# Early gathers behind splits, spread rows, first gates in two parts, and single-head routing in a transformer block with an expert layer

## The chip, the cores and the metric

The kernel runs on one core of one Trainium2 chip. The metric is the device time of one execution in microseconds; a kernel's time is the median of several. The engines are named as in the profile: PE is TensorE (matmul), DVE is VectorE, ACT is ScalarE, POOL is GpSimd, SP is SyncE, which here only issues DMAs.

## The reference

One residual block on x of 512 tokens by 1024 columns, all in float32. The first half (a gated MLP on token blocks and a banded attention, added to x through `w_out`) isn't touched by the change. The second half is a layer of small experts:

```
q = (xb @ w_query).reshape(128, 8, 2, 128)            # 8 heads, two halves
sc = einsum('thpd,hpkd->thpk', q, sub_keys)           # 128 keys in each half
s_top, i_top = top_k(sc, 16)
cand = s_top[0][:, None] + s_top[1][None, :]          # 256 pairs, index i0 * 128 + i1
best, pos = top_k(cand, 16);  eidx = cand_idx[pos];  g = softmax(best)
u = expert_u[eidx];  h = gelu(einsum('thkd,td->thk', u, xb))
out = einsum('thk,thkd->td', g * h, expert_v[eidx])
```

There are 128 x 128 = 16384 experts; each token takes 16 in each of 8 heads, 128 rows of `expert_u` and 128 of `expert_v`.

## The kernel before

**Two ways to the same sum.** For the first tile of 128 tokens (the gathered tile) the chosen rows are fetched with indirect DMAs, 128 gathers of u rows (L876) and 128 of v rows (L887); DVE multiplies (L878) and accumulates (L889). For the other 384 tokens (the dense tiles) all experts are computed: first products `u . x` for 128 chunks of 128 experts, gelu (`act`, L547), times a gate that is zero for experts not chosen, then second products with `expert_v`. The last 64 of the dense tokens have no first products: their 128 u rows per token are gathered early (64 gathers of 128 rows, `rowe`, L480), DVE dots them (L489), and the result goes into their gates. So first products have 320 columns and second products 384.

**Splits.** Each weight tile of 512 KB comes by a DMA on SP into `raw` (three buffers); ACT makes `hi` (L124), and DVE or POOL `lo` = raw - hi (L125). A product is three matmuls, hi by hi, hi by lo and lo by hi (L140 to L142). A k-step is the three matmuls of one of the 8 slices of 128 rows; a first product of one chunk of 128 experts takes 8 k-steps, and the kernel takes the chunks in pairs (64 pairs, numbered c; "chunk" below means a pair, and `AHEAD` = 23 and `LAST` count pairs).

**Stages.** Up to some 225 us in the profile the first half of the block. To 460 us *routing* of the dense tiles, head by head: `candidates(h)` makes q and scores on PE with weight splits on POOL, two or three first products as filling, and the top 16 keys on DVE; `pairs` and `choose` of head h-1 find the best 16 pairs (L593, L600 to L619). POOL issues the early gathers here: `indices_early` brings a head's indices into place with a DMA and a cast (`eui`, L495, L496), then `gather_early` issues up to six at a time into `rowe` buffers.

From 460 to 620 us the *gate stage*, written out by hand for PE, DVE, ACT and POOL: 48 steps of 8 tokens. In each, DVE compares an iota with the second index (`bm`, L747), POOL multiplies by the gate (L749), DVE and ACT compare with the first index (`am`, L757, L761, L763), and two steps later PE multiplies the two (L770, 16 matmuls in the profile, shown as x8 in the order): the result is the gate of all 16384 experts for these tokens. ACT copies it into `gst` (L773), and after every second step a store of 1 MB goes from ACT's queue to DRAM (`gd<-gst`, L776, 24 in all). Until step 32 each step also issues one early gather on POOL and dots one row on DVE as long as there are any; in the profile these are 22. Between the products PE works at k-steps of first products, as many as are left up to chunk `AHEAD - LAST`, spread evenly over the steps that are left, rounded up; their tiles are split as they are used.

Then the *passage*: the remaining first products up to chunk 23, and for the first chunk of second products the gates' load from DRAM (`gc<-gd`, L910, 1536 KB for 8 chunks of 128 experts, issued by POOL; later ones by SP), `act` times gate on DVE (L923, in place), `wh` and `wl` (L924, L925; L934 and L935 for the 64 columns that come straight from the gates) and the matmuls L945, L946 and L949.

To the end the *second product*: 64 chunks, PE's order by hand, with the first products of chunk c+23 behind chunk c. At every sixth chunk `route_gathered` selects for two heads of the gathered tile (`PARTS` = 4; scores `s0d` by a DMA into `sc0`, top 16 on DVE, the tree copied by POOL at L600), and the gathers and their DVE work are spread over the chunks, with four buffers `row`, of which each selection takes one as well.

**Order.** Outside the parts by hand a scheduler sets each engine's order from the order of the program, priorities and buffers; `tc.issue_after(x)` keeps what is inside behind instruction x. An engine takes its instructions strictly in order, and so does each queue of DMAs.

Of the kernel before, what the change touches and what calls it, by code (L numbers as in the profile page):

```python
# [8 lines left out]
F32 = mybir.dt.float32  # L9
# [5 lines left out]
ALU = mybir.AluOpType  # L15
# [4 lines left out]
P = 128  # L20
D = 1024
# [5 lines left out]
NH = 8  # L27
TOPK = 16
# [27 lines left out]
RAW = 3  # L56
HI = 5
LO = 5
ROW = 4
ROWA = 6  # L60
ROWE = 4
LAGE = 3
BRIDGE = 8
EARLY = 6
LEAD = 2
ON_ACT = 2
AHEAD = 23
LAST = 3
HELD = 2
SOME = 15  # L70
FILL = (2, 2, 2, 2, 3, 3, 3, 3)
DELAY = 6
SLACK = 4
PRIO = 400
PARTS = 4
ROUTE = 6
GB = 8
TC = 8
TG = 16
NG = NDT // TG  # L80


def bcast_rows(ap, n):
# [4 lines left out]
def hybrid_block(tc, x, ln1, w_in, gng, wsT, bsb, qkg, bias, w_out, ln2, wq, skT, uT, ud, vd, out):  # L88
    nc = tc.nc
    ctx = ExitStack()  # L90
    with ctx:
# [19 lines left out]
        nc.gpsimd.iota(iota_k, pattern=[[1, P]], base=0, channel_multiplier=0,  # L111
                       allow_small_or_imprecise_dtypes=True)

        loads = []

        def load_split(src, eng=nc.vector, **dims):

            raw = big("raw", F32, RAW)
            hi = big("hi", F32R, HI)
            lo = big("lo", F32R, LO)  # L120
            fold = (lambda v: v.rearrange("p (a b) -> p a b", **dims)) if dims else (lambda v: v)
            load = nc.sync.dma_start(fold(raw), src)
            loads[:] = [getattr(load, "ins", load)]
            nc.scalar.activation(hi, raw, AF.Copy)  # L124
            eng.tensor_tensor(lo, raw, hi.bitcast(F32), op=ALU.subtract)  # L125
            return fold(hi), fold(lo)

        def chunk_of(w, c, ch=CH, eng=nc.vector):
# [337 lines left out]
        row = rq.tile([P, D], F32, name="rowe", tag="rowe", bufs=ROWA)  # L466
# [9 lines left out]
        def gather_early(n, rows_of, n_rows):  # L476

            for j in early[:n]:
                row = rows_of.tile([P, D], F32, name="rowe", tag="rowe", bufs=n_rows)
                nc.gpsimd.indirect_dma_start(out=row, out_offset=None, in_=ud,  # L480
                                             in_offset=bass.IndirectOffsetOnAxis(ap=eui[:, j:j + 1], axis=0))
                issued.append((j, row))
            del early[:n]
# [14 lines left out]
        def ready_early(h):  # L498
            early.extend(range(h * HK, (h + 1) * HK))
# [42 lines left out]
        def multiply_tile(whole=False):  # L542
            multiply_some(KT, whole)
# [122 lines left out]
        def indices_of(t):  # L666

            ei = gat.tile([P, NH * TOPK], I32, name="ei", tag="ei", bufs=1)
            ii = gat.tile([P, 2, NH * TOPK], I32, name="ii", tag="ii", bufs=1)
            ff = gat.tile([P, 2, NH * TOPK], F32, name="ff", tag="ff", bufs=2)  # L670
# [8 lines left out]
            pass  # L679
        cands = []  # L680
        for h in range(NH + 1):
            if h > 1:
                ready_early(h - 2)
            dots_early(0)
            gather_early(EARLY, rq, ROWA)
            if h < NH:
                cands.append(candidates(h))
            else:
                for i, _ in enumerate(first_products(sum(FILL) + BC, BRIDGE, nc.gpsimd, True)):
                    behind.append(done[0])  # L690
            if h > 0:
                hs = slice((h - 1) * TOPK, h * TOPK)
                ps = pa()
                mask = ps[:, 0:6 * ND * TOPK].bitcast(U32)
                tree = rq.tile([P, ND, TOPK, 32], F32, name="tree", tag="tree", bufs=1)
                with tc.issue_after(behind[BRIDGE // 2 - 1]) if behind else ExitStack():
                    cand = pairs(rq, *cands.pop(0), ND, ps[:, 6 * ND * TOPK:8 * ND * TOPK])
                choose(rq, cand, ND, gate[:, GT:, hs], eidx[:, GT:, hs], mask, tree, nc.scalar.copy)
                indices_early(h - 1)
            if h == 4:  # L700

                nc.gpsimd.tensor_copy(xch, xbh[:, :, T0:T0 + NDU])
                nc.gpsimd.tensor_copy(xcl, xbl[:, :, T0:T0 + NDU])
# [10 lines left out]
            split_next()  # L714
        with tc.issue_after(behind[-3]):
            softmax(rq, gate[:, GT:, :].rearrange("p t (h k) -> p (t h) k", k=TOPK), ND * NH)
        ready_early(NH - 1)
        dots_early(0)
        routing.close()
        xn_ctx.close()  # L720


        gd = dram.tile([NB // GB, P, NG, GB * TG], F32, name="gd")
        more.append(ctx.enter_context(tc.tile_pool(name="more", bufs=1)))
        gp_ctx = ExitStack()
        gp = gp_ctx.enter_context(tc.tile_pool(name="gp", bufs=1))
# [46 lines left out]
                nc.scalar.copy(st[:, :, t0:t0 + 4], ps.rearrange("p (t b) -> p b t", b=NB))  # L773

        def store(n, st):
            nc.scalar.dma_start(gd[:, :, n, :].rearrange("q p f -> p q f"),  # L776
                                st.rearrange("p (q b) t -> p q (b t)", b=GB))

        def rows_of_v(c):

# [7 lines left out]
        engines = {getattr(mybir.EngineType, e) for e in ("PE", "DVE", "Activation", "Pool")}  # L788
        own = steps - UX // TC
        with tc.manual_schedule(engines=engines):  # L790
            multiply_tile()
            gs[0] = gates_of(GT, ff.pop(0))
            split_next()
            multiply_tile()
            for n in range(steps + LEAD):
                t, c = divmod(n, per)
                if n < steps:
                    bms[n] = second_one_hot(gs[t], c)
                if n >= LEAD:
                    m = n - LEAD  # L800
                    if m * TC % TG == 0:
                        st = gp.tile([P, NB, TG], F32, name="gst", tag="gst", bufs=2)
                    products(ams.pop(m), bms.pop(m), m % per, st)
                    if (m + 1) * TC % TG == 0:
                        store(m * TC // TG, st)
                while begun:
                    activate_tile()
                if n < steps:
                    ams[n] = first_one_hot(gs[t], c)
                if n < own - 7:  # L810
                    gather_early(1, gp, ROWE)
# [12 lines left out]
                if n == own - 3:  # L824

                    late = gates_of(GT + t, ff.pop(t))
                if n == own - 1:
                    gs[t] = late

                made = len(ready) * KT + (KT - open_tile[4] if open_tile else 0)  # L830
                left = (AHEAD - LAST) * BC * KT - split * KT + made
                some = -(-left // (steps + LEAD - n))
                multiply_some(some)
                while split < (AHEAD - LAST) * BC + HELD and len(ready) < HELD:
                    split_next(nc.vector if split % 2 else nc.gpsimd)
# [10 lines left out]
        gat_ctx.close()  # L846


        ep = ctx.enter_context(tc.tile_pool(name="ep", bufs=1))

        xb0 = ep.tile([P, D], F32, name="xb0")
        nc.gpsimd.dma_start(xb0, xbd[0])
        acc0 = ep.tile([P, D], F32, name="acc0")
# [2 lines left out]
        def route_gathered(b):  # L856
# [5 lines left out]
            for h in range(n):  # L862
                for p2 in range(2):
# [3 lines left out]
            mask = ep.tile([P, 6 * n * TOPK], U32, name="mask", tag="mask", bufs=1)  # L867
            tree = ep.tile([P, D], F32, name="tree", tag="row", bufs=ROW)
            choose(ep, pairs(ep, top, pos, n), n, best, to, mask,
                   tree.rearrange("p (h k m) -> p h k m", h=n, k=TOPK))  # L870
            softmax(ep, best, n)
            nc.vector.tensor_copy(eint[:, hs], eidx[:, 0, hs])

# [29 lines left out]

        acx = px()
        accs = [[acx[:, 0:512], acx[:, 512:]]] + [[pa() for _ in range(2)] for _ in range(ND - 1)]
        gcs = {}

        def load_gates(q, eng):
            gcs[q] = ep.tile([P, NG, GB, TG], F32, name="gc", tag="gc", bufs=2)
            eng.dma_start(gcs[q].rearrange("p n b t -> p (n b t)"), gd[q].rearrange("p n f -> p (n f)"))  # L910

        def second_product(c):
            w = weights.pop(c) if c in weights else rows_of_v(c)
            if c == 0:
                load_gates(0, nc.gpsimd)
# [105 lines left out]
```

## Time and profile before

| | |
|---|---|
| median of 3 runs | 1485.53 us (1485.14 to 1485.57) |
| the profiled execution | 1489.41 us |
| its span, first to last instruction | 1487.5 us |
| mean granted PE clock | 0.983 |
| busy PE, DVE, POOL, ACT | 1410.3, 1143.3, 682.8, 651.7 us |
| DMA moved | 396.77 MB |

The profile is one execution on the chip. A busy time counts each engine's own instructions; idle time is put down to the instruction or DMA that ended it. Names are those of the program's buffers: `lo<-raw,hi` is an instruction that writes `lo` and reads `raw` and `hi`. The prediction shows the lines that it uses. PE matmuls overlap, so that the time from one start to the next tells what one costs, not its length.

### The profile page before, as it was taken

The numbers are of one execution on the slowest core, as the hardware profiler recorded it, in microseconds if no ns is written. First come the engines' busy times: TensorE is split into PE (matmuls) and PEld (weight loads), VectorE is DVE, ScalarE is ACT, GpSimd is POOL, SyncE is SP. The second block draws the span as 40 slices with busy tenths as digits, with TensorE's granted clock in tenths as the row PEclk, the third lists the DMA queues.
The fourth block names the chain that finished last, engine by engine and source line by source line (L and its number), as shares of the span: only waits on it lengthen the run. The fifth ranks groups of instructions, "written<-read, shape, count | busy, mean of one in ns | idle before, by whom it ended". The sixth has DMA issues, their size and how long they took to land.

```text
span 1487.5 us, 21777 instructions
## 1 busy us (share of the span) xinstructions
PE 1410.3 (95%) x7804; PEld 1238.6 (83%) x7804; DVE 1143.3 (77%) x2397; ACT 651.7 (44%) x1124; POOL 682.8 (46%) x464
## 2 busy tenths in 40 slices
PE   7999999999889878889989999999999999999998
PEld 6886688998788778888978888888989999888877
DVE  4437543698987979588989879898898888788783
ACT  5447534443345667643434334343343333433331
POOL 0000007577776877404435455465465544444430
PEclk9999999999989999999999999999999999999999
DMA  5352136387765986868879899999999999889892
GB/s 184 114 184 71 61 111 201 131 285 259 260 211 163 333 283 199 244 224 326 302 280 338 300 357 341 337 355 344 379 349 358 359 332 372 333 287 325 319 365 94
DMA packets 161419, 396.77 MB, mean 267 GB/s; under 512 B 12304, under 2 KB 74528, under 8 KB 159264
## 3 DMA queue, kind: packets, MB, share of 16 engines
q1 hardware_dynamic: 62992, 197.42, 37.4%
q0 software_dynamic: 47488, 171.50, 31.3%
q10 hardware_dynamic: 50832, 26.48, 6.2%
q8 instruction: 61, 1.00, 0.3%
q14 instruction: 46, 0.38, 0.1%
HBM read 363.86 MB, written 31.46 MB: 266 GB/s over the span
## 4 chain that ended last, share of the span: by engine, by line
PE 48%; DMA 17%; DVE 11%; issue 10%; POOL 8%; ACT 4%; ACTq 0%; SPq 0%; DVEq 0%; POOLq 0%
PE pu L140 7%; PE pu L142 7%; PE pu L141 7%; DMA row<-in_vd,eint 4%; PE pa L945 4%; PE pa L946 4%; PE pa L949 4%; DMA row<-in_ud,eint 3%; DMA raw<-in_uT 3%; DVE lo L125 3%; POOL lo L125 3%; DMA gc<-gd 3%; PE pa L140 2%; PE pa L142 2%; PE pa L141 2%
## 5 line engine op out<-in xcount | busy, mean ns | idle before, releaser
L124 ACT ACTIVATE hi<-raw 128x1024 fp32r<-128x1024 f32 x300 | 316.9, 1059 | 551.1 <-DMA raw<-in_vd 239.2
L125 DVE TENSOR_TENSOR lo<-raw,hi 128x1024 fp32r<-128x1024 f32 x249 | 305.0, 1226 | 107.9 <-ACT hi L124 106.8
L887 POOL DMA_INDIRECT row<-in_vd,eint x128 | 197.4, 1542 | 184.3 <-DVE acc L889 158.8
L876 POOL DMA_INDIRECT row<-in_ud,eint x128 | 185.9, 1452 | 202.8 <-DVE row L878 146.5
L140 PE MATMUL pu<-xch,hi 128*128 128x320 f32 x784 | 248.2, 317 | 2.4 <-ACT act L547 2.3
L142 PE MATMUL pu<-xch,lo 128*128 128x320 f32 x784 | 242.8, 310 | 0.8 <-DVE lo L125 0.6
L141 PE MATMUL pu<-xcl,hi 128*128 128x320 f32 x784 | 242.9, 310 | 0.0
L945 PE MATMUL pa<-hi,wh 128*128 128x512 f32 x512 | 200.6, 392 | 0.0
L946 PE MATMUL pa<-lo,wh 128*128 128x512 f32 x512 | 200.0, 391 | 0.0
L889 DVE SCALAR_TENSOR_TENSOR acc<-row,hw,acc 128x1024 f32<-128x1024 f32 x128 | 164.9, 1288 | 43.2 <-DMA row<-in_vd,eint 42.9
L878 DVE SCALAR_TENSOR_TENSOR row<-row,xb 128x1024 f32<-128x1024 f32 x128 | 155.7, 1218 | 31.3 <-DMA row<-in_ud,eint 31.2
L125 POOL TENSOR_TENSOR lo<-raw,hi 128x1024 fp32r<-128x1024 f32 x51 | 123.5, 2435 | 81.5 <-ACT hi L124 76.8
L949 PE MATMUL pa<-hi,wl 128*128 128x512 f32 x512 | 157.7, 389 | 0.0
L140 PEld LDWEIGHTS pu<-xch,hi 128*128 128x128 f32 x784 | 148.8, 190 | 5.9 <-ACT act L547 4.4
L142 PEld LDWEIGHTS pu<-xch,lo 128*128 128x128 f32 x784 | 148.5, 189 | 1.9 <-DVE lo L125 1.3
L141 PEld LDWEIGHTS pu<-xcl,hi 128*128 128x128 f32 x784 | 148.8, 190 | 1.4
L770 PE MATMUL pa<-bm,am 128*128 128x128 f32 x768 | 105.1, 291 | 27.3 <-POOL bm L749 12.7
L770 PEld LDWEIGHTS pa<-bm,am 128*128 128x128 f32 x768 | 97.6, 203 | 34.7 <-POOL bm L749 26.0
L945 PEld LDWEIGHTS pa<-hi,wh 128*128 128x128 f32 x512 | 96.7, 189 | 20.6
L946 PEld LDWEIGHTS pa<-lo,wh 128*128 128x128 f32 x512 | 96.6, 189 | 20.4
L949 PEld LDWEIGHTS pa<-hi,wl 128*128 128x128 f32 x512 | 96.3, 188 | 20.5
L946 PE MATMUL px<-lo,wh 128*128 128x512 f32 x256 | 101.6, 397 | 7.9 <-DVE lo L125 7.9
(218 smaller groups left out, 2664.1 us busy)
## 6 DMA issues: line engine op xcount, KB each, us to landing
raw<-in_uT SPq DMA_DIRECT2D x128, 512.0 KB, 5.8
raw<-in_vd SPq DMA_DIRECT2D x128, 512.0 KB, 5.6
gd<-gst ACTq DMA_DIRECT2D x24, 1024.0 KB, 6.6
gc<-gd SPq DMA_DIRECT2D x15, 1536.0 KB, 10.7
raw<-in_w_in SPq DMA_DIRECT2D x20, 512.0 KB, 4.5
raw<-in_wq SPq DMA_DIRECT2D x16, 512.0 KB, 3.7
raw<-in_w_out SPq DMA_DIRECT2D x8, 512.0 KB, 4.2
bt<-in_bias SPq DMA_DIRECT2D x8, 256.0 KB, 7.3
```

What stands on the lines that cost most here:

```text
L124: nc.scalar.activation(hi, raw, AF.Copy)
L125: eng.tensor_tensor(lo, raw, hi.bitcast(F32), op=ALU.subtract)
L140: nc.tensor.matmul(ps, lh[0], rh[0], start=first, stop=False)
L141: nc.tensor.matmul(ps, lh[0], rh[1], start=False, stop=False)
L142: nc.tensor.matmul(ps, lh[1], rh[0], start=False, stop=last)
L770: nc.tensor.matmul(ps[:, i * P:(i + 1) * P], am[:, 4 * q + i, :], bm[:, 4 * q + i, :], start=True, stop=True)
L876: nc.gpsimd.indirect_dma_start(out=row, out_offset=None, in_=ud, in_offset=bass.IndirectOffsetOnAxis(ap=eint[:, j:j + 1], axis=0))
L887: nc.gpsimd.indirect_dma_start(out=row, out_offset=None, in_=vd, in_offset=bass.IndirectOffsetOnAxis(ap=eint[:, j:j + 1], axis=0))
L889: nc.vector.scalar_tensor_tensor(acc0, row, hw[:, j:j + 1], acc0, op0=ALU.mult, op1=ALU.add)
L945: nc.tensor.matmul(accs[t][half], wh[:, b, tok], w[b][0][:, ds_], start=first, stop=False)
L946: nc.tensor.matmul(accs[t][half], wh[:, b, tok], w[b][1][:, ds_], start=False, stop=False)
L949: nc.tensor.matmul(accs[t][half], wl[:, b, tok], w[b][0][:, ds_], start=False, stop=last)
```

## The change

It has five parts.

1. *Gathers behind splits.* In the routing loop the index DMA and cast and the early gathers of head h-2 are placed behind the first POOL split of head h (`splits`), where before the gathers stood ahead of it in the program and the indices at the end of the turn before. All `rowe` buffers now come from one pool with six buffers; before the gate stage had four of its own. One gather is issued ahead of the gate stage. `pairs` and `choose` of the last head wait for different first products.
2. *Gate-stage rows spread.* A gather is issued in two of three steps up to step 32, not in every one until none is left.
3. *`LAST` 3 to 2.* One chunk more, two tiles of 8 k-steps, gets its first products within the gate stage, and the passage has as many fewer.
4. *First gates.* The stored gates are two DRAM tensors, groups 0 to 19 (the 320 columns) and 20 to 23. The first block's large part (1280 KB) is loaded from POOL at step 46 into memory that comes free at step 39; the small part (256 KB) after the last stores. All later blocks are two loads on SP as well. The two buffers `gc` are in two pools.
5. *Single heads and five buffers.* `PARTS` 8 and `ROUTE` 3: one head at every third chunk. `ROW` 5.

```diff
-ROW = 4
+ROW = 5
-LAST = 3
+LAST = 2
-PARTS = 4
-ROUTE = 6
+PARTS = 8
+ROUTE = 3
+GROUPS = ((0, NDU // TG), (NDU // TG, NG))
...
-            if h > 1:
-                ready_early(h - 2)
             dots_early(0)
-            gather_early(EARLY, rq, ROWA)
             if h < NH:
                 cands.append(candidates(h))
...
+            if h > 1:
+                with tc.issue_after(splits[0]):
+                    indices_early(h - 2)
+                    ready_early(h - 2)
+                    gather_early(EARLY, gat, ROWA)
...
-                indices_early(h - 1)
...
+        def load_gates(q, eng, parts=range(len(GROUPS))):
+            if q not in gcs:
+                gcs[q] = gcp[q % 2].tile([P, NG, GB, TG], F32, name="gc", tag="gc", bufs=1)
+            for i in parts:
+                n0, n1 = GROUPS[i]
+                eng.dma_start(gcs[q][:, n0:n1].rearrange("p n b t -> p (n b t)"),
+                              gds[i][q].rearrange("p n f -> p (n f)"))
...
-                if n < own - 7:
-                    gather_early(1, gp, ROWE)
+                if n < own - 7 and n % 3 < 2:
+                    gather_early(1, gat, ROWA)
...
                 if n == own - 1:
                     gs[t] = late
+
+                    gat_ctx.close()
+                    gcp = [ctx.enter_context(tc.tile_pool(name="gcp", bufs=1, side="right"))]
+                if n == steps - 2:
+                    load_gates(0, nc.gpsimd, range(1))
...
+        gcp.append(ep)
+
+        load_gates(0, nc.gpsimd, range(1, len(GROUPS)))
```

Line numbers of the changed kernel are a few higher: L480 is L482 there, L495 is L497, L770 is L775, L910 is L792, L923 is L938, L924 is L939.

**POOL in routing, fourth to sixth block of early gathers.** Before, from the fourth index DMA on (`lo` is a split, `rowe` a gather):

```order
L495 DMA eui<-eidx 64x8
L496 CAST eui<-eidx 64x8
L480 DMA rowe<-in_ud,eui 128x1024 x6
L125 TENSOR_TENSOR lo<-raw,hi 128x1024
L480 DMA rowe<-in_ud,eui 128x1024 x2
L125 TENSOR_TENSOR lo<-raw,hi 128x1024 x3
L495 DMA eui<-eidx 64x8
L496 CAST eui<-eidx 64x8
L125 TENSOR_TENSOR lo<-raw,hi 128x1024
L480 DMA rowe<-in_ud,eui 128x1024 x4
```

Now, from the same index DMA on:

```order
L497 DMA eui<-eidx 64x8
L498 CAST eui<-eidx 64x8
L125 TENSOR_TENSOR lo<-raw,hi 128x1024
L482 DMA rowe<-in_ud,eui 128x1024 x6
L125 TENSOR_TENSOR lo<-raw,hi 128x1024 x3
L497 DMA eui<-eidx 64x8
L498 CAST eui<-eidx 64x8
L125 TENSOR_TENSOR lo<-raw,hi 128x1024 x2
L482 DMA rowe<-in_ud,eui 128x1024 x6
L125 TENSOR_TENSOR lo<-raw,hi 128x1024 x3
```

The first three blocks (6 and 2, 8, and 8 gathers, each behind one split) stand the same in both; in the fourth the six gathers went from ahead of a split to behind it, in the fifth behind two. In all, 43 gathers now stand ahead of the gate stage's steps, 42 before.

**PE in the gate stage, at the thirteenth to fifteenth step's products.** Before, one k-step between the products of two steps (`pa` is a gate product, `pu` a first product):

```order
L770 MATMUL pa<-bm,am 128x128 x8
L140 MATMUL pu<-xch,hi 128x320
L141 MATMUL pu<-xcl,hi 128x320
L142 MATMUL pu<-xch,lo 128x320
L770 MATMUL pa<-bm,am 128x128 x8
```

Now, at the same place:

```order
L775 MATMUL pa<-bm,am 128x128 x8
L142 MATMUL pu<-xch,hi 128x320
L143 MATMUL pu<-xcl,hi 128x320
L144 MATMUL pu<-xch,lo 128x320
L142 MATMUL pu<-xch,hi 128x320
L143 MATMUL pu<-xcl,hi 128x320
L144 MATMUL pu<-xch,lo 128x320
L775 MATMUL pa<-bm,am 128x128 x8
```

Two k-steps stand behind the first 12 products before and behind the first 28 now, one behind the others: 16 k-steps moved. Behind the last product, 30 k-steps and one matmul stand ahead of the first L945 before, and 17 k-steps now.

**DVE in the passage.** Before, behind the last `am`:

```order
L125 TENSOR_TENSOR lo<-raw,hi 128x1024 x4
L923 TENSOR_TENSOR act<-act,gc 128x320 x2
L935 TENSOR_TENSOR wl<-gc,wh 128x4x2x16
L923 TENSOR_TENSOR act<-act,gc 128x320 x4
L925 TENSOR_TENSOR wl<-act,wh 128x2x320
```

Now, at the same place:

```order
L938 TENSOR_TENSOR act<-act,gc 128x320 x8
L125 TENSOR_TENSOR lo<-raw,hi 128x1024 x2
L940 TENSOR_TENSOR wl<-act,wh 128x2x320 x2
L125 TENSOR_TENSOR lo<-raw,hi 128x1024
L950 TENSOR_TENSOR wl<-gc,wh 128x4x2x16 x2
```

The products with the gates went ahead of the splits. On ACT, two `wh`, an `act` and a `hi` now stand ahead of the `hi` that the first second-product matmul reads, and the `wh` for the gates' own columns behind it. On POOL the first load of gates stands ahead of the last `bm` and the second directly behind it. `wh` and `wl` lie in memory that `gst` had before, and so wait for the last stores. DVE has 1793 instructions in its order, 1712 before; SP 208, 187 before.

More of the change, by code (lines that the diff above doesn't have):

```diff
@@ L58 @@
 LO = 5
-ROW = 4
+ROW = 5
 ROWA = 6
-ROWE = 4
 LAGE = 3
@@ L112, in hybrid_block @@
                        allow_small_or_imprecise_dtypes=True)
-        loads = []
+        loads, splits = [], []
         def load_split(src, eng=nc.vector, **dims):
@@ L124, in load_split @@
             nc.scalar.activation(hi, raw, AF.Copy)
-            eng.tensor_tensor(lo, raw, hi.bitcast(F32), op=ALU.subtract)
+            ins = eng.tensor_tensor(lo, raw, hi.bitcast(F32), op=ALU.subtract)
+            if eng is nc.gpsimd:
+                splits[:] = [getattr(ins, "ins", ins)]
             return fold(hi), fold(lo)
@@ L465, in hybrid_block @@
         rq = routing.enter_context(tc.tile_pool(name="rq", bufs=1))
-        row = rq.tile([P, D], F32, name="rowe", tag="rowe", bufs=ROWA)
+        row = gat.tile([P, D], F32, name="rowe", tag="rowe", bufs=ROWA)
         for i in range(P // UX):
@@ L669, in indices_of @@
             ii = gat.tile([P, 2, NH * TOPK], I32, name="ii", tag="ii", bufs=1)
-            ff = gat.tile([P, 2, NH * TOPK], F32, name="ff", tag="ff", bufs=2)
+            ff = gat.tile([P, 2, NH * TOPK], F32, name="ff", tag="ff", bufs=1)
             nc.scalar.copy(ei, eidx[:, t, :])
@@ L695, in hybrid_block @@
                 tree = rq.tile([P, ND, TOPK, 32], F32, name="tree", tag="tree", bufs=1)
+                with tc.issue_after(behind[BRIDGE // 2 - 2]) if behind else ExitStack():
+                    cand = pairs(rq, *cands.pop(0), ND, ps[:, 6 * ND * TOPK:8 * ND * TOPK])
                 with tc.issue_after(behind[BRIDGE // 2 - 1]) if behind else ExitStack():
-                    cand = pairs(rq, *cands.pop(0), ND, ps[:, 6 * ND * TOPK:8 * ND * TOPK])
-                choose(rq, cand, ND, gate[:, GT:, hs], eidx[:, GT:, hs], mask, tree, nc.scalar.copy)
-                indices_early(h - 1)
+                    choose(rq, cand, ND, gate[:, GT:, hs], eidx[:, GT:, hs], mask, tree, nc.scalar.copy)
             if h == 4:
@@ L716, in hybrid_block @@
             softmax(rq, gate[:, GT:, :].rearrange("p t (h k) -> p (t h) k", k=TOPK), ND * NH)
+        indices_early(NH - 1)
         ready_early(NH - 1)
@@ L720, in hybrid_block @@
         xn_ctx.close()
-        gd = dram.tile([NB // GB, P, NG, GB * TG], F32, name="gd")
+        gds = [dram.tile([NB // GB, P, n1 - n0, GB * TG], F32, name=f"gd{n0}") for n0, n1 in GROUPS]
         more.append(ctx.enter_context(tc.tile_pool(name="more", bufs=1)))
@@ L775, in store @@
         def store(n, st):
-            nc.scalar.dma_start(gd[:, :, n, :].rearrange("q p f -> p q f"),
+            gd, (n0, n1) = next((g, r) for g, r in zip(gds, GROUPS) if n < r[1])
+            nc.scalar.dma_start(gd[:, :, n - n0, :].rearrange("q p f -> p q f"),
                                 st.rearrange("p (q b) t -> p q (b t)", b=GB))
+        gcs = {}
+        def load_gates(q, eng, parts=range(len(GROUPS))):
[5 more added lines that the diff above has]
+                              gds[i][q].rearrange("p n f -> p (n f)"))
         def rows_of_v(c):
@@ L809, in hybrid_block @@
                     ams[n] = first_one_hot(gs[t], c)
-                if n < own - 7:
-                    gather_early(1, gp, ROWE)
+                if n < own - 7 and n % 3 < 2:
+                    gather_early(1, gat, ROWA)
                 dots_early(LAGE)
@@ L845, in hybrid_block @@
         gp_ctx.close()
-        gat_ctx.close()
         ep = ctx.enter_context(tc.tile_pool(name="ep", bufs=1))
+        gcp.append(ep)
+        load_gates(0, nc.gpsimd, range(1, len(GROUPS)))
         xb0 = ep.tile([P, D], F32, name="xb0")
@@ L869, in route_gathered @@
             choose(ep, pairs(ep, top, pos, n), n, best, to, mask,
-                   tree.rearrange("p (h k m) -> p h k m", h=n, k=TOPK))
+                   tree[:, 0:n * TOPK * 32].rearrange("p (h k m) -> p h k m", h=n, k=TOPK))
             softmax(ep, best, n)
@@ L905, in hybrid_block @@
         accs = [[acx[:, 0:512], acx[:, 512:]]] + [[pa() for _ in range(2)] for _ in range(ND - 1)]
[L906 to L910, printed above, removed]
         def second_product(c):
             w = weights.pop(c) if c in weights else rows_of_v(c)
-            if c == 0:
-                load_gates(0, nc.gpsimd)
             gc = gcs[c * BC // GB]
```

## The prediction

> **What bounds the kernel now.** I read the page first, then a table of busy time by stretch, then waits and single rows in the stretches where TensorE (PE) is not full. The page's first row says which engine counts:
>
> ```profile
> PE 1410.3 (95%) x7804; PEld 1238.6 (83%) x7804; DVE 1143.3 (77%) x2397; ACT 651.7 (44%) x1124; POOL 682.8 (46%) x464
> ```
>
> PE is busy for 95% of 1487.5 us, so a gain must be PE time that is now idle or runs at a lower clock. The table by stretch (columns: stretch, its length, busy us and instruction count of each engine, granted PE clock, DMA share, GB/s) says where that is:
>
> ```profile
> 360.00:400.00 40.00, 34.84 (x183) 30.51 (x182) 36.61 (x163) 12.66 (x22) 28.59 (x22) 0.96 0.71 244
> 400.00:440.00 40.00, 34.06 (x198) 32.70 (x197) 35.38 (x165) 15.45 (x25) 30.55 (x21) 0.87 0.78 253
> 460.00:500.00 40.00, 32.38 (x231) 30.16 (x230) 33.57 (x41) 26.28 (x60) 35.56 (x23) 0.96 0.84 269
> 500.00:540.00 40.00, 32.82 (x229) 30.23 (x229) 38.19 (x49) 26.19 (x62) 35.43 (x25) 0.91 1.01 323
> 580.00:620.00 40.00, 33.74 (x265) 32.24 (x264) 29.52 (x30) 31.29 (x74) 28.77 (x15) 0.96 0.72 206
> 620.00:645.00 25.00, 20.65 (x122) 20.20 (x121) 12.72 (x19) 11.48 (x18) 2.37 (x4) 0.86 0.79 279
> 740.00:780.00 40.00, 35.50 (x188) 31.36 (x188) 35.03 (x92) 12.71 (x18) 15.88 (x11) 0.96 0.79 288
> 980.00:1480.00 500.00, 498.60 (x2550) 436.78 (x2549) 406.77 (x520) 183.97 (x260) 233.44 (x155) 1.00 0.89 329
> ```
>
> From 980 us on nothing is to be had: 498.6 of 500. The change has four places to work in: the late routing (360 to 440, 11.1 us idle), the gate stage (460 to 620), the passage to the second product (620 to 645) and that product's first third.
>
> **First gates loaded ahead, 16 k-steps moved (LAST 3 to 2).** These are the rows of PE, ACT and DVE around the passage; the bracket is the idle time before the row and what ended it. The last two are from the list of DMAs of 600 to 640, KB each and us to landing at their end.
>
> ```profile
> 620.35 0.39 PE L140 MATMUL pu<-xch,hi 128*128 128x320 f32 x1
> ...
> 633.63 0.30 PE L140 MATMUL pu<-xch,hi 128*128 128x320 f32 x1
> 638.29 0.79 PE L945 MATMUL px<-hi,wh 128*128 128x512 f32 x1 [4.35 <-ACT wh L924]
> 621.24 0.37 ACTq L776 DMA_DIRECT2D gd<-gst  x1
> 637.51 0.72 ACT L924 ACTIVATE wh<-act 128x640 fp32r<-128x640 f32 x1
> 638.14 0.30 ACT L934 ACTIVATE wh<-gc 128x128 fp32r<-128x128 f32 x1
> 635.91 0.89 DVE L923 TENSOR_TENSOR act<-act,gc 128x320 f32<-128x320 f32 x2 [4.99 <-DMA gc<-gd]
> gd<-gst ACTq DMA_DIRECT2D x4, 1024.0 KB, 5.4
> gc<-gd POOLq DMA_DIRECT2D x1, 1536.0 KB, 8.3
> ```
>
> The gates' products end at 620.35, which I call X. A k-step of a first product is three matmuls; PE's order has 30 1/3 of them ahead of the first L945, from 620.35 to the last, begun at 633.63: 0.44 us each. Then it waits to 638.29, 4.5 us, because the gates load cannot start before the last store lands and takes 8.3.
>
> After the change the large part needs only stores 0 to 19 and stands on POOL ahead of the last bm. Two steps ahead of X, at 3.3 each (48 steps from 460 to 620), that is X-6 or before; with 8.3 us it lands by X+2.3, and act*gc is done by X+5.9 (eight, 0.89 for two). Then wh still waits: its memory is that of the last stores, issued at X+0.9 and 5.4 in the air, X+6.3. Two wh (0.63 from start to start), an act and a hi (1.05) stand ahead of the first L945, so it starts at X+8.9. PE arrives with 17 k-steps at X+7.5: a stall of 1.4, so 3.1 us less. The small load follows the last stores at X+6.5; at the stores' 5.4 it is there at X+11.9, while PE wants its columns three k-steps and twelve matmuls of 0.2 (498.6 by 2550) after X+8.9, at X+12.6: nothing, up to 2 us.
>
> After a stall the clock counts:
>
> ```profile
> 376.00:382.00 6.00, 3.27 (x24) 2.82 (x24) 5.24 (x32) 4.86 (x7) 4.48 (x6) 1.00 0.80 255
> 388.00:392.00 4.00, 1.57 (x9) 1.23 (x8) 3.76 (x10) 2.38 (x7) 4.00 (x3) 0.97 0.91 340
> 392.00:396.00 4.00, 4.00 (x12) 3.09 (x12) 4.00 (x18) 1.38 (x2) 2.24 (x1) 0.60 0.85 266
> 642.00:644.00 2.00, 2.00 (x10) 2.00 (x9) 1.25 (x2) 1.04 (x3) 0.00 (x0) 0.50 0.69 217
> 644.00:646.00 2.00, 2.00 (x10) 1.74 (x10) 2.00 (x4) 0.00 (x0) 0.00 (x0) 0.91 0.26 70
> ```
>
> After 4.5 us PE ran at half clock from 638.3 to 644, which loses 3.0 us. After the 2.4 us idle of 388 to 392 it lost 0.4 of 4 us, 1.6 (0.60); the two waits within 376 to 382 left it at 1.00. A stall of 1.4 should therefore keep the clock: 3.0 us gained. The Trainium skill, page "TensorE: Matmul & The Clock Gate", Part 1, gives about 3.4 us of idle as what drops the array to half; here 2.4 us was enough, so the trace draws the line lower. By the page a left-over stall of 2 to 3 us would cost no clock, by the rows 1.6 us more; the sum for 1.4 us is the same by both.
>
> The 16 k-steps (7.0 us) leave the passage for products 12 to 27, which get two k-steps where they had one. Do they fit there? Group rows of 460 to 621:
>
> ```profile
> L749 POOL TENSOR_TENSOR bm<-bm,gt 128x1024 f32<-128x1024 f32 x48 | 90.9, 1899 | 23.9 <-DVE bm L747 22.3
> L747 DVE TENSOR_TENSOR bm<-iota_k,pa 128x1024 f32<-128x1024 f32 x48 | 58.2, 1213 | 10.7 <-PE pa L770 6.9 <-ACT ni L738 3.3
> L773 ACT COPY gst<-pa 128x512 f32<-128x512 f32 x96 | 52.7, 581 | 28.6 <-PE pa L770 20.8 <-DMA gd<-gst 7.8
> L757 DVE TENSOR_TENSOR am<-iota_k,pa 128x768 f32<-128x768 f32 x48 | 45.3, 944 | 0.0
> L489 DVE SCALAR_TENSOR_TENSOR rowe<-rowe,px 128x1024 f32<-128x1024 f32 x22 | 26.4, 1209 | 0.0
> L480 POOL DMA_INDIRECT rowe<-in_ud,eui x22 | 21.7, 987 | 3.3 <-issue 1.6
> 618.64 1.95 PE L770 MATMUL pa<-bm,am 128*128 128x128 f32 x16
> ```
>
> PE needs at most 1.95 + 2 x 0.44 = 2.83 us for such a step. DVE needs 1.21 + 0.94 + 1.21 = 3.4 where a row is dotted, 2.2 where not; two of three with rows make 3.0. So PE just fits below DVE: I take 2 us of the 7.0 as visible (0 to 7.0), which includes two more tiles to split. Sum of this part: 3.1 + 3.0 + 7.0 - 2 = 11 us gained (4 to 14).
>
> **Gate-stage rows spread.** The work of POOL and DVE is unchanged: 22 gathers of 0.99, 22 dots of 1.21. Bounded step by step, 22 steps of 3.4 and 26 of 2.2 cost as much in any order, so the average gives nothing. What can go is contention: DMA stands at 1.01 in 500 to 540, and ACT waits 7.8 us for stores. By the table's instruction counts PE does 229 against 265 matmuls per 40 us early and late; bringing the first 80 us half-way there would give 5, but gathers now reach into steps that had none. I take 3 (from 9 gained to 4 lost).
>
> **Gathers behind splits.** POOL and ACT in the block that has changed order:
>
> ```profile
> 370.84 0.56 POOL L495 DMA_DIRECT2D eui<-eidx  x1 [0.80 <-DVE top L562]
> 375.07 1.01 POOL L480 DMA_INDIRECT rowe<-in_ud,eui  x1 [3.44 <-DMA eui<-eidx]
> 382.38 2.41 POOL L125 TENSOR_TENSOR lo<-raw,hi 128x1024 fp32r<-128x1024 f32 x1
> 389.58 1.06 ACT L124 ACTIVATE hi<-raw 128x1024 fp32r<-128x1024 f32 x1 [8.70 <-POOL lo L125]
> ```
>
> POOL waits 3.44 for the indices' DMA and then issues six gathers up to 382.38, while a split could run; ACT later waits 8.70 for POOL, and PE the 2.4 of 388 to 392. With the lo first it lies inside the 3.44, and the others come 2.4 us earlier: that stall goes, with its 1.6 of clock. The first three blocks of gathers stand as before, and what else is idle in 400 to 440 lies beside a DVE that is busy for 35.38 of 40. I take 4, from 11 (all idle of 360 to 440) to 4 lost (one more stall as long as the passage's 4.35).
>
> **Single heads, five row buffers.** In the second product PE waits for splits on DVE, and DVE for gathered rows:
>
> ```profile
> 764.13 1.28 DVE L889 SCALAR_TENSOR_TENSOR acc<-row,hw,acc 128x1024 f32<-128x1024 f32 x1 [4.91 <-DMA row<-in_vd,eint]
> PE px L946 <- DVE lo L125: 7.9, 4, 3.5
> L607 DVE TENSOR_SCALAR mask<-bpos 128x32 uint32<-128x32 uint32 x24 | 2.5, 172 | 0.0
> ```
>
> A fifth buffer lets each gather start one row sooner, so the wait of 4.91 shrinks, and PE's longest one behind it (3.5) with it. Against it DVE has 81 more instructions; at 0.17 each, the narrow ones' duration, 14 us at most, half of it made up by narrower rows, in stretches where DVE is 35.0 of 40. I take 3 gained (9 gained, 8 lost). The gates' second, 256 KB load per block is not waited for by PE, which is full from 980: nothing. The Trainium skill, "DMA: Bandwidth & Descriptors", Rules for kernel authors, speaks against such splitting and asks for 1 MiB or more per DMA; no wait of PE here depends on it.
>
> **The sum.** 11 + 3 + 4 + 3 = 21 us. The profiled execution took 1489.4 with its ends: 1468.4. The median of the runs shown lies 3.9 below it, hence 1464.5.
>
> **Rivals.**
> - *Only the passage gains.* Spread, routing and single heads cancel; DVE's 35 to 36 of 40 in routing speaks for it. 1485.5 - 11 = 1474.5.
> - *It does not do what it says.* On DVE act*gc now stands ahead of two splits. If the large load lands after X+8, as it would at the old start, those splits and PE wait for it, stall and half clock stay, and the moved k-steps show in full: 7.0 - 7.0, so 1485.5. For it speaks that the load shares the DMA with the last stores.
> - *Slower: DVE stops at early rows.* In the late routing the gathers come behind one to three splits of 2.4 us more, while their dots on DVE stand among the next head's selection rows. DVE now waits 13.0 us there:
>
> ```profile
> DVE rowe L489 <- DMA rowe<-in_ud,eui: 13.0, 14, 1.7
> ```
>
>   Four blocks of up to 7.2 add up to 29; DVE's slack of 360 to 440 (8.0) and the passage's 11 pay for 19 of it; 10 us worse, about 1495. It decides once that wait passes 32 us. Against it: the moved gathers no longer compete with splits two rows later.
>
> **How the numbers follow.** Forecast 0.60, passage alone 0.22, nothing 0.08, slower 0.10. The terms' free ends, put together as independent, are 11 better and 17 worse than the forecast; somewhat wider for what no row shows, that is 1449 below, and above it reaches to the case of nothing, 1487. A measurement can tell about 0.2%, 3 us, from no change. Faster 0.82, same 0.08, slower 0.10.
>
> **What would show it.** Right: the load of gates issued before the last gate product; first L945 some 9 us after it instead of 17.9; clock 1.00 behind it; ACT's wait of 8.70 on POOL gone; DVE's 4.91 wait shorter. Wrong: a gate stage over 163 us, DVE's wait for rowe above 30, or PE's waits for lo in 640 to 980 above their 7.9.

## The result, and the profile after

The changed kernel takes 1461.1 us (median of 4 runs, 1457.8 to 1463.0), the kernel before 1485.3 beside it: a ratio of 0.984, interval 0.982 to 0.985. That is 24 us or 1.6% faster. The forecast was 1464.5. The sum came out nearly right and its terms did not, so the profile after is read by stage. Its span is 1461.3 us, 26.2 shorter than before.

The stages are cut at five starts on PE: the first gate product, the last one (X), the first second-product matmul, and chunks 1 and 24 of the second product. These are the last two in the kernel before (lines of PE in order of time: start, length):

```profile
664.35 0.40 PE L945 MATMUL px<-hi,wh 128*128 128x512 f32 x1
...
1033.42 0.40 PE L945 MATMUL px<-hi,wh 128*128 128x512 f32 x1
```

and in the changed one, where L945 is L960:

```profile
656.12 0.40 PE L960 MATMUL px<-hi,wh 128*128 128x512 f32 x1
...
1008.91 0.40 PE L960 MATMUL px<-hi,wh 128*128 128x512 f32 x1
```

So that stretch fell from 369.1 to 352.8 us. All stages, in us, with a second profile of the same changed kernel that was taken later; the first column is the time from the span's start, the others are stretches:

| | first gate product | to X | X to first L945 | X to chunk 1 | chunk 1 to 24 | chunk 24 to 63 |
|---|---|---|---|---|---|---|
| before | 464.6 | 155.7 | 18.0 | 44.0 | 369.1 | 440.8 |
| changed | 463.3 | 156.4 | 9.5 | 36.5 | 352.8 | 438.8 |
| changed, again | 462.0 | 155.6 | 9.0 | 32.5 | 354.8 | 438.8 |

The first column says little of the change: the untouched first half alone ends 2.7 us earlier in the second profile of the same kernel than in the first (the last section shows why). Three fifths of the gain, 16.3 us, lie in the first third of the second product, where 3 were expected. DVE's waits in the kernel before, for the whole run (total, times, longest):

```profile
DVE acc L889 <- DMA row<-in_vd,eint: 42.9, 26, 4.9
DVE row L878 <- DMA row<-in_ud,eint: 31.2, 27, 5.0
```

The same two rows after the change:

```profile
DVE acc L912 <- DMA row<-in_vd,eint: 1.1, 3, 0.6
DVE row L901 <- DMA row<-in_ud,eint: 0.7, 2, 0.5
```

74 us of waiting became 2; 42 of the 74 lie between chunks 1 and 24. The table by stretch shows the same from DVE's side: before, DVE worked 319.65 of 369 us (columns as in the prediction),

```profile
664.00:1033.00 369.00, 358.08 (x1938) 319.36 (x1937) 319.65 (x609) 140.88 (x204) 183.20 (x124) 0.99 0.88 323
```

and in the changed kernel it works 329.58 of the 349 us from the same point on, with PE full:

```profile
664.00:1013.00 349.00, 347.70 (x1917) 313.93 (x1916) 329.58 (x675) 148.75 (x216) 193.05 (x130) 1.00 0.93 349
```

The passage is as forecast in its mechanism. Rows of ACT, POOL, DVE and PE of the changed kernel:

```profile
613.03 0.61 POOL L792 DMA_DIRECT2D gc<-gd  x1
620.30 3.31 DVE L938 TENSOR_TENSOR act<-act,gc 128x320 f32<-128x320 f32 x8 [6.01 <-DMA gc<-gd]
626.48 1.36 ACT L939 ACTIVATE wh<-act 128x640 fp32r<-128x640 f32 x2 [3.13 <-DMA gd<-gst]
629.16 0.50 PE L960 MATMUL px<-hi,wh 128*128 128x512 f32 x1 [1.74 <-ACT hi L124]
643.20 1.28 ACT L628 ACT_TABLE_LOAD   x1
645.67 1.28 ACT L549 ACT_TABLE_LOAD   x1
647.46 0.63 PE L142 MATMUL pu<-xch,hi 128*128 128x320 f32 x1 [2.60 <-ACT act L549]
```

The load is issued 6.6 us ahead of X, wh waits for the last store (`gd<-gst`) through its memory, and PE stops for 1.74 us instead of 4.35. The last three rows were not forecast: the first single head is selected so early that its softmax changes ACT's tables within the passage, and PE waits 2.60 us for an activation behind them. In the second profile the same two loads stand at 638.64 and 641.12, and PE waits only 0.80 us. Around both stalls of the first profile the clock (columns as above) reads

```profile
628.00:630.00 2.00, 0.84 (x5) 0.79 (x6) 1.66 (x3) 1.11 (x2) 1.11 (x3) 1.00 0.78 231
630.00:632.00 2.00, 2.00 (x12) 1.78 (x11) 0.37 (x1) 0.00 (x0) 0.00 (x0) 1.00 1.05 391
648.00:650.00 2.00, 2.00 (x9) 2.00 (x8) 2.00 (x5) 1.11 (x2) 0.00 (x0) 0.50 0.93 302
```

1.00 behind the stall of 1.74 us and 0.50 behind that of 2.60.

In the gate stage and the late routing little moved. The rows that answer to those before:

```profile
360.00:400.00 40.00, 38.41 (x211) 34.16 (x211) 37.00 (x178) 12.84 (x24) 29.02 (x20) 1.00 0.65 228
400.00:440.00 40.00, 32.43 (x201) 31.71 (x200) 34.73 (x177) 18.17 (x31) 27.76 (x20) 0.91 0.61 203
460.00:500.00 40.00, 34.05 (x254) 32.74 (x253) 31.34 (x36) 28.04 (x64) 34.42 (x23) 0.96 0.84 259
500.00:540.00 40.00, 34.59 (x258) 32.71 (x257) 34.81 (x41) 28.76 (x67) 31.28 (x20) 0.96 0.95 293
580.00:620.00 40.00, 34.29 (x268) 33.15 (x269) 27.24 (x28) 30.18 (x74) 27.69 (x16) 0.96 0.75 221
740.00:780.00 40.00, 40.00 (x228) 36.33 (x227) 39.83 (x93) 14.77 (x22) 24.71 (x17) 1.00 0.95 350
```

360 to 400 gained 3.6 us of PE work, 400 to 440 gave 1.6 back. In the gate stage PE now does 254 to 268 matmuls in 40 us early and late, but these counts hold the moved k-steps. Of gate products alone there are 170, 184, 192 and 224 in the four stretches from 460 to 620, where there were 149, 184, 216 and 221: the first stretch gained, and the third, where a second k-step now stands behind each product, lost.

### The profile page after: what moved, and what is told of

It reads as the page before. It is cut to its first block, busy times and chain, and to the rows that moved or that the text cites. A ratio compares the mean times of both kernels' runs of the same rounds, so it can differ in the third digit from the quotient of the medians.

```text
span 1461.3 us, 21818 instructions
## 1 busy us (share of the span) xinstructions
PE 1398.3 (96%) x7804; PEld 1233.7 (84%) x7804; DVE 1146.3 (78%) x2496; ACT 664.9 (46%) x1144; POOL 688.8 (47%) x470
## 4 chain that ended last, share of the span: by engine, by line
PE 52%; DVE 6%; DMA 3%; POOL 3%; ACT 2%; issue 2%; DVEq 0%; ACTq 0%; SPq 0%; POOLq 0%
PE pa L960 7%; PE pa L961 7%; PE pa L964 7%; PE pu L142 6%; PE pu L143 6%; PE pu L144 6%; PE px L960 4%; PE px L961 3%; PE px L964 3%; PE pa L775 3%; POOL bm L754 2%; DVE lo L125 1%; DMA sc<-s0d 1%; DMA raw<-in_uT 1%; DVE bm L752 1%
## 5 line engine op out<-in xcount | busy, mean ns | idle before, releaser
L899 POOL DMA_INDIRECT row<-in_ud,eint x128 | 201.2, 1572 | 177.5 <-DVE acc L912 123.8
L910 POOL DMA_INDIRECT row<-in_vd,eint x128 | 181.0, 1414 | 171.9 <-DVE row L901 117.2
L960 PE MATMUL pa<-hi,wh 128*128 128x512 f32 x512 | 199.7, 390 | 0.0
L775 PE MATMUL pa<-bm,am 128*128 128x128 f32 x768 | 102.2, 288 | 23.7 <-POOL bm L754 11.1
L775 PEld LDWEIGHTS pa<-bm,am 128*128 128x128 f32 x768 | 95.7, 200 | 29.8 <-POOL bm L754 26.1
L960 PEld LDWEIGHTS pa<-hi,wh 128*128 128x128 f32 x512 | 96.1, 188 | 20.3
L960 PE MATMUL px<-hi,wh 128*128 128x512 f32 x256 | 100.3, 392 | 1.7 <-ACT hi L124 1.7
```

Of the source, the lines that this page charges most:

```text
L775: nc.tensor.matmul(ps[:, i * P:(i + 1) * P], am[:, 4 * q + i, :], bm[:, 4 * q + i, :], start=True, stop=True)
L910: nc.gpsimd.indirect_dma_start(out=row, out_offset=None, in_=vd, in_offset=bass.IndirectOffsetOnAxis(ap=eint[:, j:j + 1], axis=0))
L960: nc.tensor.matmul(accs[t][half], wh[:, b, tok], w[b][0][:, ds_], start=first, stop=False)
```

## The experiments

Theory B: the second product gained by the fifth row buffer. Rival H: by single heads. Rival P: by the earlier end of the passage. Times are medians with their range; the ratio to the kernel before, measured beside it, has its 95% interval behind it.

**Four buffers in the changed kernel.**

```diff
-ROW = 5
+ROW = 4
```

> The changed kernel with four row buffers in place of five; single heads stay. From chunk 1 to chunk 24 of the second product the changed kernel took 352.8 us, the kernel before 369.1. Theory B (the fifth buffer made this gain, since DVE's waits for gathered rows fell from 74 us to 2): the stretch is back near 369 and the time near 1477. Theory H (it was the selection by single heads, which holds up DVE's queue for shorter at a time): 353 and 1461. Both in part: between.

1476.3 us (1472.5 to 1479.6), ratio 0.992 (0.989 to 0.995); chunk 1 to 24 takes 369.4. DVE's waits are back:

```profile
DVE acc L912 <- DMA row<-in_vd,eint: 39.4, 30, 2.9
DVE row L901 <- DMA row<-in_ud,eint: 26.2, 23, 3.5
```

As theory B has it, within a microsecond: without the fifth buffer the stretch's gain is gone.

**Single heads alone, in the kernel before.**

```diff
-PARTS = 4
-ROUTE = 6
+PARTS = 8
+ROUTE = 3
...
-                   tree.rearrange("p (h k m) -> p h k m", h=n, k=TOPK))
+                   tree[:, 0:n * TOPK * 32].rearrange("p (h k m) -> p h k m", h=n, k=TOPK))
```

> The kernel before with one edit: single heads at every third chunk (PARTS 8, ROUTE 3), four row buffers. Theory B: chunk 1 to 24 stays at 369 and the time at 1485, DVE still waits some 70 us for rows. Theory H: 353 and 1469.

1496.3 us (1489.3 to 1499.0), ratio 1.007 (1.004 to 1.009): slower than the kernel before by some 10 us, which neither theory had. Chunk 1 to 24 takes 374.8, and the wait for rows stays:

```profile
DVE acc L889 <- DMA row<-in_vd,eint: 43.0, 30, 4.7
DVE row L878 <- DMA row<-in_ud,eint: 30.9, 25, 4.1
```

H falls. Single heads without the buffer cost time: of the 10 us, 5.7 lie between chunks 1 and 24 and 3.8 behind.

**Single heads and the fifth buffer, in the kernel before.** The edit above and `ROW = 5`.

> The kernel before with single heads and five row buffers, nothing else of the change. Theories B and H: chunk 1 to 24 takes 353, the time is 1469, DVE's waits for rows are below 5 us. Rival P (the stretch is faster only because the passage ends earlier and in another phase): it stays at 369 and 1485.

1468.5 us (1464.9 to 1470.4), ratio 0.987 (0.984 to 0.990); chunk 1 to 24 takes 353.8, with the old passage (X to chunk 1 45.2). P falls.

```profile
DVE row L878 <- DMA row<-in_ud,eint: 1.4, 3, 0.6
DVE acc L889 <- DMA row<-in_vd,eint: 1.0, 2, 0.6
```

So the fifth buffer is worth 28 us where heads are single already (1496.3 to 1468.5), and 15 in the changed kernel. Two heads with five buffers need 1.8 KB per partition more than the kernel before has left; so single heads are what makes room for the buffer, and 10 us is what they cost without it. Two heads with five buffers were not run, so what single heads cost beside five buffers stays open. Part 5 alone gives 17 of the 24 us; the other four parts add 7 with five buffers (1468.5 to 1461.1), but 20 with four (1496.3 to 1476.3). The parts do not add up singly.

**Selections one chunk later.**

```diff
-                if c % ROUTE == 0 and c < PARTS * ROUTE:
+                if c % ROUTE == 1 and c < PARTS * ROUTE:
```

> The changed kernel with the selections at chunks 1, 4, 7 and so on, no longer at 0, 3, 6. In the changed kernel PE stops for 2.8 us at 644.6, before a first product whose activation stands behind two table loads of ACT (1.28 us each) for the softmax of the first selection, and runs at half clock afterwards. If the selection in the first chunk is the cause, that stall goes or moves to where PE is not short, and the time falls by 3 to 4 us to 1457; if any first softmax stalls PE like this wherever it stands, the time stays within 1 us of the changed kernel's.

1461.7 us (1459.2 to 1464.9), ratio 0.983 (0.980 to 0.986): no change. But the edit did not move what it was to move. Only PE's order is by hand here, and the first selection's table loads still begin at X+22.8, against X+23.5 and X+21.1 in the two profiles of the changed kernel; of the eight selections only the fifth and the last came clearly later, by their softmaxes. PE waits 0.21 us behind these loads, 2.60 and 0.80 in the unedited kernel, and the stretches (34.3 to chunk 1, 355.8 from there to 24) are near those of its second profile (32.5, 354.8). So whether the selection in the first chunk causes the stall stays untested; its size varies without any edit.

**The k-steps back in the passage.**

```diff
-LAST = 2
+LAST = 3
```

> The changed kernel with LAST back at 3, so that the 16 k-steps (7.0 us) stand behind the last gate product again. If the gate stage hides them, as predicted (2 of 7 visible), the stage from the first to the last gate product is 1 to 2 us shorter than the changed kernel's 156.4, the first second-product matmul comes some 13.5 us after the last gate product without a stall (9.5 in the changed kernel, 1.9 of it stall), and the time is 1464 to 1466. If the stage pays for them in full, it is 7 us shorter, 149, and the time is 1459.

1465.6 us (1463.9 to 1467.7), ratio 0.986 (0.984 to 0.989). The time is that of the first case, the stage nearly that of the second: 150.0 us, so the stage does pay 6.4 of the 7.0. But the passage grows by more than 7: X to chunk 1 takes 48.6, and PE stops three times in it:

```profile
622.36 0.64 PE L142 MATMUL pu<-xch,hi 128*128 128x320 f32 x1 [2.42 <-ACT act L549]
632.14 0.50 PE L961 MATMUL px<-lo,wh 128*128 128x512 f32 x1 [1.46 <-DVE lo L125]
655.64 0.42 PE L142 MATMUL pu<-xch,hi 128*128 128x320 f32 x1 [3.70 <-ACT act L549]
```

**A gather in every step.**

```diff
-                if n < own - 7 and n % 3 < 2:
+                if n < own - 7:
```

> The changed kernel with an early gather in every step of the gate stage until none is left, as before, in place of two of three. Prediction (spreading relieves the DMA engines, 3 us): the stage takes 159 to 160 us, not 156.4, and the time is 1464. Rival (only the sum of DVE's and POOL's work counts, so its order does not): 156.4 within 1 us and 1461.

1464.7 us (1462.7 to 1468.7), ratio 0.986 (0.984 to 0.988). The time is the prediction's, but the stage takes 156.8, as in the rival; the profile's extra time lies ahead of the first gate product (466.4 against 463.3), where the order of every engine is the same in both. Repeats of one kernel vary by that much (the changed kernel once more: 1456.5 to 1465.1), so with the k-steps in the stage the spread shows no gain.

**Gathers ahead of splits again.** The block under `issue_after(splits[0])` is taken out, `ready_early(h - 2)` and `gather_early` stand ahead of `candidates(h)`, `indices_early(h - 1)` at the end of the turn.

> The changed kernel with the indices and early gathers of the routing loop back in their old places, ahead of the splits; the row buffers stay shared. Prediction: PE's stall of 2.4 us behind ACT's wait for POOL is back in the fourth block, the first gate product comes 4 us later than the changed kernel's 463.3, and the time is 1465. Rival (DVE sets the pace of the late routing, and the stall only changes its place): 463 to 464.5 and 1461 to 1462.

1462.7 us (1458.7 to 1464.0), ratio 0.984 (0.981 to 0.986). The time is the rival's. POOL's old order is back, but the stall is not: PE stops for 1.10 us before 390.79 where 2.4 were forecast, and ACT has no wait for POOL there. The first gate product comes at 466.0. Counted from the start of routing (the first `pa<-ident,xs` behind its wait of 2.1 us) it is 243.6 us, 1.9 longer than the longest of the ten profiles with the changed routing (238.2 to 241.7). But the three profiles with the routing of the kernel before have 236.7 to 240.6, so the old order as such is not slower. A gain ahead of the gate stage can be told neither here nor in the time.

**Both parts of the first gates loaded behind the stage, as was meant.**

```diff
-                if n == steps - 2:
-                    load_gates(0, nc.gpsimd, range(1))
...
-        load_gates(0, nc.gpsimd, range(1, len(GROUPS)))
+        load_gates(0, nc.gpsimd)
```

> The changed kernel with both parts of the first gates loaded after the gate stage; they are still stored apart. Prediction: the first second-product matmul comes when the load has landed, about 17 us after the last gate product (9.5 in the changed kernel), PE stops for some 9 us and runs at half clock behind it for 6 us, and the time is 1461 + 7.5 + 3 = 1471. Rival (the last stores' landing holds the passage anyway): 9.5 and 1461.

1471.3 us (1467.2 to 1477.1), ratio 0.991 (0.988 to 0.994): the number forecast, by another mechanism. X to the first second-product matmul is 9.1, and the gate stage takes 164.6. Freed from the order written by hand, the load went four steps ahead of the stage's end, and the products with the gates went into DVE's queue ahead of four steps' bm:

```profile
611.60 3.30 DVE L936 TENSOR_TENSOR act<-act,gc 128x320 f32<-128x320 f32 x8 [7.14 <-DMA gc<-gd]
614.82 1.21 DVE L752 TENSOR_TENSOR bm<-iota_k,pa 128x1024 f32<-128x1024 f32 x1
```

DVE stood still for 7.14 us and PE for 7.9. By its time alone it would have passed as proof.

**One tensor, loaded behind the last store.** As the last edit, and

```diff
-GROUPS = ((0, NDU // TG), (NDU // TG, NG))
+GROUPS = ((0, NG),)
```

> The changed kernel with the gates stored in one tensor again and the first block's single load behind the last store, since the kernel with two late loads did not test this: there the order put the load four steps ahead of the stage's end. Now the load can't stand ahead, because it reads what the last store writes. Prediction: the gate stage takes 156 to 157 us as in the changed kernel, the first second-product matmul comes 16 to 18 us after the last gate product (9.5 in the changed kernel), of which PE stands still for 8 to 10, the clock is near 0.5 for 6 us behind it, and the time is 1461 + 7.5 + 3 = 1471. Rival (the last stores hold the passage anyway, through the memory of wh): 10 us and 1462.

1477.4 us (1471.9 to 1482.2), ratio 0.993 (0.991 to 0.995), 16 slower than the changed kernel where 10 were forecast. The first L945 comes 20.0 us after X, as PE's order now puts 31 k-steps ahead of it, 17 in the changed kernel; PE stops for 5.9 us, the clock falls to 0.50, and X to chunk 1 is 38.7. But chunk 1 to 24 takes 364.0.

**Stored apart, small part loaded first.** This keeps the two tensors and holds the large load behind the wait for the last stores:

```diff
+            load_gates(0, nc.gpsimd, (1, 0))
```

at the end of the part by hand, both other first loads taken out.

> The changed kernel with the first gates still stored apart, but both parts loaded by POOL behind its last multiplication and the small part first, so that the large part stands behind the wait for the last stores. It parts what the kernel with one tensor mixed (there 1477, X to chunk 1 38.7 us, chunk 1 to 24 364 us; in the changed kernel 36.5 and 32.5 in its two profiles, and 353 and 355). Theory L (the late start itself costs all): X to chunk 1 is 38 to 40 us, chunk 1 to 24 is again near 364, the time 1475 or more. Theory T (the late start costs the stall and the clock only, the rest belongs to the single loads of 1.5 MB): 38 to 40 and 353 to 355, the time 1464 to 1467.

1472.4 us (1470.7 to 1477.1), ratio 0.991 (0.988 to 0.994). X to chunk 1 is 37.8, chunk 1 to 24 361.3: neither case quite, nearer to L. Some 11 us are the price of this edit, of which 1 to 5 lie in the passage and 6 to 9 between chunks 1 and 24. There PE's waits add up to 7.7 us (1.3 and 3.3 in the changed kernel's profiles), 4.3 of them for activations and 3.4 for splits on DVE. One is seen in DVE's rows, where the queue stops for the scores of the next head and a split stands behind it; PE waited 2.6 us for that split:

```profile
787.95 0.29 DVE L564 MAX8 top<-sc 128x8 f32<-128x128 f32 x1 [3.23 <-DMA sc<-s0d]
788.16 0.81 DVE L938 TENSOR_TENSOR wl<-act,wh 128x640 fp32r<-128x640 f32 x1
788.88 1.28 DVE L910 SCALAR_TENSOR_TENSOR acc<-row,hw,acc 128x1024 f32<-128x1024 f32 x1
790.08 1.22 DVE L125 TENSOR_TENSOR lo<-raw,hi 128x1024 fp32r<-128x1024 f32 x1
```

The kernel with the old passage and five buffers has no such loss (353.8), so lateness alone does not explain it. The edit also changed orders: PE has 31 k-steps ahead of the first L945 again, and DVE's queue in these chunks differs. How much is whose stays open.

**Three one-hots on ACT.**

```diff
-ON_ACT = 2
+ON_ACT = 3
```

> The changed kernel with three of the eight first one-hots of a step on ACT, no longer two. In the gate stage DVE is busy for 130 of 160 us and ACT for 117. If DVE sets the stage's pace, its am is shorter by 0.15 us in 48 steps: the stage takes 149 to 153 us instead of 156.4 and the time is 1455 to 1458. If the waits between engines set it, the longer chain on ACT (0.55 us more in each step) costs as much as is saved: 156 or more, and 1461 or above.

1465.7 us (1464.2 to 1466.0), ratio 0.985 (0.983 to 0.988). The stage takes 161.4 us, 5 more, although DVE has less to do: DVE's share alone does not set its pace, the chain through ACT counts too.

**The changed kernel again.**

> The changed kernel itself, for a comparison on the same chip with the two others and a second profile of it: 1458 to 1463, chunk 1 to 24 in 353 us, the gate stage in 155 to 157.5 us, the first second-product matmul 9 to 10 us after the last gate product.

1461.1 us (1456.5 to 1465.1), ratio 0.982 (0.980 to 0.985), its stages in the table above. No version that was tried is faster.

## Why the prediction was right, and where not

**The passage: right.** The first L945 was put at X+8.9 and came at 9.5 and 9.0; the stall at 1.4 and came at 1.7 in the profile; the cause of what is left, wh waiting for the last stores, is in the row; the clock stayed at 1.00. That last point was near the edge: the same stall is 1.98 us in the kernel with four buffers and 2.06 in the one with later selections, and half clock followed both. The large load landed before X+0.7, where DVE's products with the gates begin, so the case of nothing did not come. X to chunk 1 fell by 7.6 us in one profile and 11.5 in the other. The 13.1 of stall, clock and moved k-steps, before the price in the stage, were too many by the new stall at ACT's table loads: 2.60 and the half clock behind it in the first profile, 0.80 in the second.

**The 16 k-steps under DVE's cover: the step failed in its reason.** "So PE just fits below DVE" would leave the stage at its length whatever else is in it. Measured, the stage is as long as before with the k-steps (156.4, 155.6 against 155.7), but 6.4 shorter without them. A gather in every step with the k-steps gives 156.8; in every step without them, which is the kernel before, 155.7. So without the k-steps the spread is worth about 6 us, and with them nothing; the k-steps fill what the spread frees. Each of the four is one or two profiles, and kernels with the same stage differ by some 3 us (154.3 to 157.5 in seven with k-steps and spread); the kernel before also has fewer `rowe` buffers. The step compared PE with DVE alone. In the changed kernel's stage PE waits longest for the `bm` that POOL has multiplied, 11.1 us in eight waits, and 7.2 for DVE's. The sum of the two terms, 3 gained less 2 lost, was measured as 0.7 lost and 0.1 gained.

**Gathers behind splits: the stall went, the gain did not come.** The stall at 388 is gone (360 to 400 is up from 34.84 to 38.41). But the sign "ACT's wait of 8.70 on POOL gone" did not come true; there is such a wait at a later split (in the second profile 3.8 us):

```profile
414.03 1.06 ACT L124 ACTIVATE hi<-raw 128x1024 fp32r<-128x1024 f32 x1 [7.22 <-POOL lo L125]
```

PE stops for 3.02 us behind it, at 415.46, where the kernel before stopped for 1.96, and then for 3.46 (3.98 before), and 400 to 440 fell from 34.06 to 32.43. The first gate product is 1.3 and 2.6 us earlier than before, but from the start of routing it is 238.2 and 239.5 us, against 239.1: the rest is the first half, which the change does not touch. So nothing of the 4 us can be told. The reason given against a larger gain, that DVE is nearly full there, may be why; no run shows that.

**Single heads and five buffers: the term that was mis-sized, 3 us against 16.3, and 2.0 more behind chunk 24.** The step priced one wait of DVE (4.91) and the one PE stall behind it, with 9 as its end. In the kernel before DVE waited 74 us in all for gathered rows, 42 of them between chunks 1 and 24. On an engine with 320 of 369 us of work, each such wait delays the splits behind it. Of the 16.3 us, 9.5 are PE's waits, which fell from 10.8 (four for `lo` with 7.9 together, three for activations) to 1.3. About 3.4 are two times half clock, behind the stalls at 767 and 849. The rest shows in no wait of PE. The price of single heads, "14 us at most, half of it made up", was fair: 10 when alone.

**The rivals.** The passage alone (1474.5) is close to what the changed kernel with four buffers does, 1476.3, but by its number only, since single heads are in that kernel too. DVE's wait for `rowe` did not grow: 13.0 before and

```profile
DVE rowe L491 <- DMA rowe<-in_ud,eui: 11.8, 10, 3.9
```

after, far from the 32 from which the slower case would have decided. So the time was right by luck, because errors cancelled: passage and stage gave 6.9 of the 14 expected in the first profile, the time up to the first gate product 1.3 of 4, the second product 18.3 of 3.

## What to carry to other kernels

Price a wait by all of it on its engine over the stretch, not by the longest one: here DVE had work for nearly nine tenths of the time, 42 us of its waits for transfers cost some 16 on PE, and one more buffer was worth 15 to 28 us, the four parts planned by hand 7 to 20. Cut a changed kernel at a few fixed instructions and compare the stages, since a sum that fits can hide terms that don't, and an experiment can give the forecast time through another mechanism. Fill and relief belong together: work moved into the gate stage was free only as far as something else in the same change made room. And look in the profile whether an edit moved what it was meant to move, since outside the parts by hand the scheduler decides.

## What the runs showed of the hardware

The length of a stall alone does not tell what it does to PE's clock. This is one and the same stall of the first half, which no edit touches, with the clock behind it, first in the changed kernel's first profile, then in its second:

```profile
146.01 1.12 PE L321 MATMUL pu<-ident,pe 128*128 128x128 f32 x4 [2.81 <-ACT pT L323]
145.65:152.48 6.83, 6.47 (x36) 4.24 (x36) 4.66 (x19) 4.41 (x14) 0.00 (x0) 0.50 0.00 1
145.66 0.71 PE L321 MATMUL pu<-ident,pe 128*128 128x128 f32 x4 [2.81 <-ACT pT L323]
145.65:152.48 6.83, 6.82 (x70) 4.60 (x70) 6.26 (x23) 5.03 (x16) 0.00 (x0) 1.00 0.02 4
```

In the clock records of the 14 profiles shown here, half clock begins at times that are multiples of 3.41 us apart within a profile, and while the kernel runs it lasts one or more such windows. What decides, as far as these traces show, is PE's busy share of the window before. Cut into such windows, the profiles have 4834 at full clock from 240 us on. All 86 in which PE was busy for less than 43% were followed by half clock, and none of those above 49%; in between both happen. The first stall above lies with 2.45 us in one window, the second is cut into 1.61 and 1.20. So the prediction's line by length, drawn between 1.4 and 2.4 us, is not one: in the kernel before, 1.96 us at 414.80 was followed by half clock and 2.30 at 608.12 was not. The passage's 1.74 left 49% of its window busy, just enough. The Trainium skill, "TensorE: Matmul & The Clock Gate", Part 1, puts the idle time at one window of about 3.4 us that runs free of the kernel; the window's length agrees, but here a window with PE busy for 40% of it was enough.

The stall shown above is 2.80 or 2.81 us long in all 14 profiles. Half clock followed it in eight, and routing starts at 224.5 to 225.5 us there; in the other six it starts at 222.1 to 222.5. The same kernel came out between 1456.5 and 1465.1 us in one series. So differences of 2 or 3 us between kernels were not read as effects of an edit. One softmax between gelus cost two table loads of 1.28 us on ACT.
